# V of the second pass in seven products, its weight factors made on GpSimd, and x columns loaded one step ahead

## The chip, the cores and the metric

The kernel runs on one core of a Trainium2 chip. The metric is the device time of one execution in microseconds (us). The engines are named as in the profile: PE (TensorE, matmuls), PEld (its weight loads), DVE (VectorE), ACT (ScalarE), POOL (GpSimd) and SP (SyncE, which here issues all DMA transfers).

## The reference

One layer of a decoder trunk over 2048 tokens of width 1024, in fp32. The input projection has 6144 columns.

```python
h = rms_norm(x, g_pre) * (1 + scale) + shift
(pv, pg, hq, hf, hi, hg, mg_pool, mg_hgrn) = split(h @ w_in)   # 512, 512, then six times 1024
branch_a = (pooled(pv) * pool_scale * silu(pg)) @ w_pool_o
f = lb + (1 - lb) * sigmoid(hf);  q = silu(hq);  v = hi         # 8 heads of 128
o = rms_norm(hgrn2(q, 1 - f, v, log f), hgrn_norm_g)            # gated linear recurrence
branch_b = (o * silu(hg)) @ w_hgrn_o
y = (sigmoid(mg_pool) * branch_a + sigmoid(mg_hgrn) * branch_b) @ w_out
x = x + gate * rms_norm(y, g_post)
```

The stage that the change is mainly about is `v = hi`: h (2048x1024) times the 1024 columns of `w_in` that begin at `O_I`, called V below.

## The kernel before

**Passes and stages.** Two passes (`p`) over 1024 tokens each; a pass has two halves `t` of T = 512 tokens, and a half four tiles `tk` of P = 128. The stages of a pass follow each other: V, eight heads (in each three groups of products, `fq`, `m` and `gp`, and the small matmuls of the recurrence, the tiles `psa`, `PT`, `K`, `X` and `sq`), the projection of branch A (`psA`), that of branch B (`psB`), and y. During y of pass 0 the h of pass 1 is made: `x_cols` loads 256 columns of x in two transfers into `xc` and scales them on DVE, and `h_in` transposes a 128-column block of them on TensorE (`xT`). These steps wait in two lists, `early` (for half 0) and `late` (half 1). Two of `early` run after each part of y, and one of `late` after each part of y's second half; what is left of `late` runs in V of pass 1.

**A product.** fp32 products are made of three products of a rounded type: `split` casts the high part on ACT and subtracts it from the whole on DVE for the low part, and three matmuls of 128x512 sum hi·hi, hi·lo and lo·hi (two letters, as `hB` and `lB`, name the two parts).

**Weights.** `items` is the list of all weight tiles in the order of use. `take()` returns the next one (`whl`), and prepares up to four ahead (`LOOK`). In pass 0 a weight is loaded (`wr`), split, and where `keep` says so stored to DRAM (`scr`); in pass 1 `again` reloads the split tile, 512 KB, in one transfer.

**Seven products.** The input h is held as combinations of its halves and row blocks (`mv`; B11, B21, B12, B22 and T1 to T4, made from h by `h_mix`, whose calls are the list `mixes`), and the products of the heads and y of pass 1 use seven products on those combinations and on combinations of the weights, where plain halves would take eight. `rows7` does it for a stage of four weight tiles for each product: per product 4 weights x 4 tiles x 3 matmuls. y of pass 1 uses it (`FAST_Y`). Its weight combinations, the row factors, are made by `row_factors` in 56 small steps: it loads two blocks of rows, makes sums on DVE, splits each factor, and stores it to `scr` in DRAM. `htick`, which is called 21 times in a head (168 times in a pass), takes a step at every second call. V of both passes is computed without that, by `v_job`: 2 halves x 2 column groups x 8 weights x 4 tiles x 3 = 384 matmuls in pass 1.

**Order.** Each engine runs its instructions in program order. All DMA issues stand in one queue, SP's, also in order, so a store that waits for its data holds back the loads behind it. A scheduler places the instructions of the stages among one another, so small changes of a duration or a wait move rows on all engines.

Of the kernel before, what the change touches and what calls it, by code (L numbers as in the profile page):

```python
# [8 lines left out]
F32 = mybir.dt.float32  # L9
# [7 lines left out]
MUL, ADD, SUB, MAX, MIN = ALU.mult, ALU.add, ALU.subtract, ALU.max, ALU.min  # L17
# [3 lines left out]
D = 1024  # L21
# [10 lines left out]
O_PV, O_PG, O_Q, O_F, O_I, O_G, O_MP, O_MH = 0, 512, 1024, 2048, 3072, 4096, 5120, 6144  # L32
# [1 line left out]
MASK_W = P + 2 * 64 + 5 * NT * 64  # L34
NU = 76
GAP = 5
FAST_V, FAST_Y = False, True
KINDS = (("m", "gp"), ("gp", "m"))


# [30 lines left out]
def tile_block(ctx: ExitStack, tc: tile.TileContext, x, c, w_ada, b_ada, g_pre, g_post, w_in,  # L71
# [20 lines left out]
    def utile(name, dt=F32):  # L92
        return up.tile([P, T], dt, tag="u", name=name)

    def dram(name, shape):
        return dp.tile(shape, F32, name=name, tag=name)
# [10 lines left out]
    def store(key, dst, src):  # L107
        last["st"] = SP.dma_start(dst, src)

    def gated(dst, src, key=None):  # L110

        with after(last["st"]):
            return SP.dma_start(dst, src)
# [55 lines left out]
    scr = {}  # L169
    ready = []  # L170

    def split(src32, hi, lo):
        return A.copy(hi, src32), V.tensor_tensor(lo, src32, hi.bitcast(F32), op=SUB)  # L173

    def raw_load(name, srcs):
        raw = wrp.tile([P, T], F32, tag="wr", name=f"wr{name}")
# [6 lines left out]
    def item_split(name, raw):  # L183
        w = item_tile(name)
        split(raw, w[:, 0:T], w[:, T:2 * T])
        return w
# [60 lines left out]
            return [f0, f1, f2, f3, lambda: one(4, "21"), lambda: one(5, "12"), lambda: one(6, "22")]  # L247
        items.append((7, make))

    def row_factors(key, src):  # L250

        steps = []
        W = T // 2
        for i in range(4):
            for c0 in (0, W):
                r = {}

                def put(f, nm, i=i, c0=c0, r=r):
                    w = utile(f"rf{key}{f}{i}{c0}", F32R)
                    hi, lo = w[:, 0:W], w[:, W:T]  # L260
                    split(r[nm], hi, lo)
                    if (key, f, i) not in scr:
                        scr[key, f, i] = dram(f"scr_{key}_{f}_{i}", [P, 2 * T])
                    store((key, f, i), scr[key, f, i].rearrange("p (z n) -> p z n", z=2)[:, :, c0:c0 + W],
                          w.bitcast(F32).rearrange("p (z n) -> p z n", z=2))

                def ld(i=i, c0=c0, r=r):
                    a, b = utile(f"ra{key}{i}{c0}"), utile(f"rb{key}{i}{c0}")
                    for w, k in ((a, 2 * i), (b, 2 * i + 1)):
                        SP.dma_start(w.rearrange("p (z n) -> p z n", z=2),  # L270
                                     src[k * P:(k + 1) * P, :].rearrange("p (z n) -> p z n", z=2)[:, :, c0:c0 + W])
                    r.update({"11": a[:, 0:W], "21": a[:, W:T], "12": b[:, 0:W], "22": b[:, W:T]})

                def sums(r=r, i=i, c0=c0):
                    r["s1"] = utile(f"rs{key}{i}{c0}")[:, 0:W]
                    tt(r["s1"], r["21"], r["22"], op=ADD)
                    tt(r["21"], r["11"], r["21"], op=SUB)

                def sums2(r=r):
                    tt(r["11"], r["s1"], r["11"], op=SUB)  # L280

                def sums3(r=r):
                    tt(r["12"], r["12"], r["11"], op=SUB)

                def two(*fs, put=put):
                    for f in fs:
                        f() if callable(f) else put(*f)
                nop = lambda: None
                steps += [ld, nop, lambda two=two: two((0, "11"), (1, "12")),
                          lambda two=two, a=sums: two(a, (2, "s1")),  # L290
                          lambda two=two, a=sums2: two(a, (3, "11")),
                          lambda two=two, a=sums3: two((4, "21"), a),
                          lambda two=two: two((5, "12"), (6, "22"))]
        return steps
# [100 lines left out]
    def poolw_setup():  # L395
        pw = utile("pw_raw")
        SP.dma_start(pw.rearrange("p (g d) -> p g d", d=P), pool_w.rearrange("g c d -> c g d"))
        split(pw, pwh, pwl)
# [43 lines left out]
    def tt(o, a, b, op=MUL, e=None):  # L442
        return (e or V).tensor_tensor(o, a, b, op=op)  # L443
# [32 lines left out]
    def x_cols(p, t, i, cx):  # L476

        cs = []
        for half in range(2):
            xc = utile(f"xc{p}_{t}_{i}_{half}")  # L480
            v = xc.rearrange("p (a n) -> p a n", n=256)
            tok = p * 8 + t * NT + half * 2
            gated(v, x[tok * P:(tok + 2) * P, i * 256:(i + 1) * 256].rearrange("(a p) n -> p a n", p=P))
            for a in range(2):
                V.tensor_scalar(v[:, a, :], v[:, a, :], rst[:, tok + a:tok + a + 1], None, op0=MUL)
            cs.append(v)
        cx["xc"][t, i] = cs

    def h_in(p, t, k, cx):

        pt_ = px.tile([P, T], F32, tag="px", name=f"xT{p}_{t}_{k}")
        for tk in range(NT):
            if (t, k // 2) in cx["xc"]:
                src = cx["xc"][t, k // 2][tk // 2][:, tk % 2, (k % 2) * P:(k % 2 + 1) * P]
            else:
                src = cx["x"][t, tk][k // 4][:, (k % 4) * P:(k % 4 + 1) * P]
            PE.transpose(pt_[:, tk * P:(tk + 1) * P], src, ident)
        h32 = utile(f"h32_{p}_{t}_{k}")
        A.activation(h32, pt_, AF.Identity, bias=shv[:, k:k + 1], scale=scv[:, k:k + 1])
        cx["h32"][t, k] = h32  # L500
        nm = ("B11", "B21", "B12", "B22")[2 * t + k % 2]
        return part(p, nm, k // 2, h32, cx)

    def part(p, nm, i, src, cx):
        hi, lo = utile(f"h{nm}{p}_{i}", F32R), utile(f"l{nm}{p}_{i}", F32R)
        cx["mv"][nm, i] = (hi, lo)
        return split(src, hi, lo)
# [676 lines left out]
    for p in range(NPASS):  # L1184
# [50 lines left out]
        psa[:] = [ph.tile([P, T], F32, tag=f"ph{i}", name=f"psa{p}_{i}") for i in range(2)]  # L1235
        behind_heads = []
        if p == 0 and FAST_V:
            behind_heads += row_factors("v7", w_in[:, O_I:O_I + D])
        if p == NPASS - 1 and FAST_Y:
            behind_heads += row_factors("y7", w_out)  # L1240
        every = [0]

        def htick():
            tick()
            every[0] += 1
            if every[0] % 2 == 0:
                once(behind_heads)

        v_head(p, 0, cx)
        for h in range(NH):  # L1250
# [17 lines left out]
            steps = []  # L1268

            def tick_in():  # L1270
                htick()
                once(steps)

            quad("fq" + n, cx, fq, htick)
            active.extend(hgrn(p, h, t, cx) for t in range(2))
            htick()
            for i, kind in enumerate(KINDS[h == NH - 1]):
                if kind == "gp":
# [28 lines left out]
        if p + 1 < NPASS:  # L1307
            nx = cxs[p + 1]
            for t, steps in ((0, early), (1, late)):
                for i in range(4):  # L1310
                    steps.append(lambda p=p, t=t, i=i, nx=nx: x_cols(p + 1, t, i, nx))
                    for k in (2 * i, 2 * i + 1):
                        steps.append(lambda p=p, t=t, k=k, nx=nx: h_in(p + 1, t, k, nx))
        if p == NPASS - 1 and FAST_Y:
            y_fast(p, cx)
        for t in range(0 if p == NPASS - 1 and FAST_Y else 2):
# [32 lines left out]
```

## Time and profile before

| | us |
|---|---|
| median of 3 runs (lowest, highest) | 1829.64 (1827.5, 1830.42) |
| the profiled execution: its own time | 1831.51 |
| its span in the profile | 1829.7 |
| granted TensorE clock, mean | 0.996 |

| stage | from (us) | to (us) |
|---|---|---|
| start and V of pass 0 | 0 | 137 |
| heads of pass 0 | 137 | 700 |
| psA, psB of pass 0 | 700 | 846 |
| y of pass 0 | 846 | 944 |
| V of pass 1 | 944 | 1034 |
| heads of pass 1 | 1034 | 1600 |
| psA, psB of pass 1 | 1600 | 1740 |
| y of pass 1 and the tail | 1740 | 1830 |

Times are from the start of the span. In a row of a group, "x" is a count; in a row of the timeline the first two numbers are start and duration, and what stands in brackets is how long the engine was idle before and who ended it.

### The profile page before, as it was taken

To read this page: it belongs to the slowest core of one execution; us is meant where nothing else is said; L and a number is where in the kernel's file an instruction comes from. 1 tells how busy PE (TensorE), PEld (TensorE's weight loads), DVE (VectorE), ACT (ScalarE), POOL (GpSimd) and SP (SyncE) were. 2 spreads that over 40 slices of the span, in tenths; PEclk is the share of its full clock that TensorE was granted. 3 is DMA by queue.
4 is the path that set the end of the run, shared out by engine and by line. 5 is a ranking of instruction groups with operands and counts; after the bars stand their busy time and mean duration, and the time that the engine had idled before them with its cause. 6 is when DMAs were issued, how large, how long until landed. Compare 5 with 4: busy or idle time off the path is not lost.

```text
span 1829.7 us, 32049 instructions
## 1 busy us (share of the span) xinstructions
PE 1772.8 (97%) x12005; PEld 1449.7 (79%) x12005; DVE 1148.9 (63%) x2460; ACT 826.9 (45%) x1939; POOL 77.6 (4%) x136
## 2 busy tenths in 40 slices
PE   5899999999999999999999999999999999999997
PEld 4788878788788787887788878888788788888885
DVE  7577887787888884565443266566566555623446
ACT  4655656556666572223322345455455354310032
POOL 1100000000000100000000000000000000000001
PEclk9999999999999999999999999999999999999998
DMA  8698676777767669987887776876876755695457
GB/s 301 207 321 289 219 271 231 253 253 242 259 236 255 238 222 320 353 304 258 303 293 255 267 256 208 288 259 212 285 238 215 237 179 189 202 348 190 137 208 275
DMA packets 255540, 460.98 MB, mean 252 GB/s; under 512 B 20077, under 2 KB 129306, under 8 KB 255386
## 3 DMA queue, kind: packets, MB, share of 16 engines
q1 hardware_dynamic: 255386, 458.95, 73.1%
q8 instruction: 94, 1.54, 0.3%
q14 instruction: 60, 0.49, 0.1%
HBM read 271.70 MB, written 187.17 MB: 251 GB/s over the span
## 4 chain that ended last, share of the span: by engine, by line
PE 79%; ACT 5%; DMA 4%; DVE 4%; POOL 2%; issue 2%; SPq 0%; POOLq 0%; DVEq 0%; ACTq 0%
PE psB L325 9%; PE psV L325 8%; PE pagp L325 7%; PE pafq L325 7%; PE pam L325 5%; PE pefq L325 5%; PE psA L325 4%; PE pegp L325 4%; PE psy L325 3%; PE pem L325 3%; PE psa L325 3%; PE pbfq L325 2%; PE pdfq L325 2%; PE pdm L325 2%; PE pbm L325 2%; PE pbgp L325 2%
## 5 line engine op out<-in xcount | busy, mean ns | idle before, releaser
L173 DVE TENSOR_TENSOR whl<-wr,whl 128x512 fp32r<-128x512 f32 x210 | 144.1, 690 | 85.7 <-ACT whl L173 84.4
L173 ACT CAST whl<-wr 128x512 fp32r<-128x512 f32 x210 | 130.0, 620 | 127.7 <-PE psB L325 26.5
L325 PE MATMUL psV<-whl,hB 128*128 128x512 f32 x512 | 162.6, 400 | 1.4 <-ACT V L840 1.4
L325 PE MATMUL psB<-Gh,whl 128*128 128x512 f32 x512 | 158.6, 390 | 0.0
L325 PEld LDWEIGHTS psV<-whl,hB 128*128 128x128 f32 x512 | 97.7, 193 | 21.5 <-ACT V L840 1.7
L631 DVE COPY_PREDICATED PT<-mask,psa 128x256 f32<-128x256 uint8 x160 | 86.2, 548 | 44.3 <-PE psa L325 44.2
L325 PEld LDWEIGHTS psB<-Gh,whl 128*128 128x128 f32 x512 | 96.1, 188 | 20.4 <-issue 0.5
L325 PE MATMUL psV<-whl,lB 128*128 128x512 f32 x256 | 101.2, 397 | 0.0
L325 PE MATMUL psB<-Gl,whl 128*128 128x512 f32 x256 | 100.0, 391 | 0.0
L325 PE MATMUL pam<-hT,whl 128*128 128x512 f32 x256 | 87.4, 402 | 0.0
L325 PE MATMUL pagp<-hT,whl 128*128 128x512 f32 x256 | 86.2, 397 | 0.0
L325 PE MATMUL psA<-Ph,whl 128*128 128x512 f32 x256 | 82.6, 397 | 3.4 <-DMA Ph<-Pd 1.7
L325 PE MATMUL pafq<-hT,whl 128*128 128x512 f32 x256 | 84.0, 389 | 0.0
L443 DVE TENSOR_TENSOR K<-K,TT 128x256 f32<-128x256 f32 x192 | 81.4, 425 | 0.7 <-PE psa L325 0.7
L325 PE MATMUL psy<-whl,mgh 128*128 128x512 f32 x256 | 80.6, 395 | 0.7 <-DVE y L443 0.7
L325 PEld LDWEIGHTS psa<-X,K 128*32 128x32 f32 x2816 | 50.0, 110 | 30.0 <-issue 19.2
L325 PE MATMUL psa<-X,K 128*32 128x48 f32 (+2 forms) x2816 | 60.7, 208 | 2.7 <-DVE PT L625 2.7
L443 DVE TENSOR_TENSOR sm<-psB,sm 128x512 f32<-128x512 f32 x32 | 22.0, 688 | 63.8 <-PE psB L325 62.4
L625 DVE COPY_PREDICATED PT<-mask,psa 128x256 f32<-128x256 uint8 (+1 forms) x96 | 52.0, 542 | 12.0 <-PE psa L325 11.9
L325 PEld LDWEIGHTS psA<-Ph,whl 128*128 128x128 f32 x256 | 47.6, 188 | 15.0 <-DMA Ph<-Pd 3.5
L325 PEld LDWEIGHTS psV<-whl,lB 128*128 128x128 f32 x256 | 49.1, 192 | 10.5
L325 PEld LDWEIGHTS pagp<-hT,whl 128*128 128x128 f32 x256 | 48.0, 188 | 10.9 <-issue 0.2
(437 smaller groups left out, 4532.2 us busy)
## 6 DMA issues: line engine op xcount, KB each, us to landing
wr<-in_w_in_dram SPq DMA_DIRECT2D x122, 256.0 KB, 4.7
whl<-scr_y SPq DMA_DIRECT2D x44, 512.0 KB, 4.7
sm<-Sd SPq DMA_DIRECT2D x64, 256.0 KB, 4.6
whl<-scr_v SPq DMA_DIRECT2D x32, 512.0 KB, 4.2
scr_y<-rfy SPq DMA_DIRECT2D x56, 256.0 KB, 3.2
wa<-in_w_ada_dram SPq DMA_DIRECT2D x32, 256.0 KB, 5.4
x<-in_x_dram SPq DMA_DIRECT2D x32, 256.0 KB, 5.4
Vd<-V SPq DMA_DIRECT2D x32, 256.0 KB, 2.4
```

The lines of the kernel that those rows point to most:

```text
L173: return A.copy(hi, src32), V.tensor_tensor(lo, src32, hi.bitcast(F32), op=SUB)
L325: PE.matmul(o, lhsT=l, rhs=r, start=start, stop=stop, skip_group_check=True)
L443: return (e or V).tensor_tensor(o, a, b, op=op)
L625: V.copy_predicated(dst.rearrange("p (c a) b -> p c a b", c=NT), m.unsqueeze(1).broadcast_to(shp), src.unsqueeze(2).broadcast_to(shp))
L631: V.copy_predicated(dst.rearrange("p (c q) a b -> p c q a b", c=NT), m, src.rearrange("p c (a b) -> p c a b", b=b).unsqueeze(2) .broadcast ...
```

## The change

It has three parts.

1. V of pass 1 is computed by `rows7`, with 336 matmuls where 384 were. Its row factors, 28 tiles of 512 KB, are made during the heads of pass 0 by `row_factors`, with the low parts and the sums on GpSimd (`G`); the casts stay on ACT. For that there are 16 loads and 56 stores of 256 KB, 56 casts on ACT, and 88 operations of 128x256 on GpSimd. The 16 stores of 512 KB by which V of pass 0 kept its split weights for pass 1 go, and the 32 reloads in V of pass 1 become 28 reloads of factors. The `mixes`, which ran one at a time through the second half of V, run within the second of the seven products (B21), and the `late` steps that are left within the first (B11).
2. `htick` takes a step of the factors at two of five calls, where it was one of two, for V's factors in pass 0 and y's in pass 1.
3. The columns of x in y of pass 0 are loaded one step ahead of the transposes that use them (`ORDER_IN`).

```diff
-FAST_V, FAST_Y = False, True
+FAST_V, FAST_Y = True, True
+ORDER_IN = ("x0", "x1", "h0", "h1", "x2", "h2", "h3", "x3", "h4", "h5", "h6", "h7")
...
-    def split(src32, hi, lo):
-        return A.copy(hi, src32), V.tensor_tensor(lo, src32, hi.bitcast(F32), op=SUB)
+    def split(src32, hi, lo, e=None):
+        return A.copy(hi, src32), (e or V).tensor_tensor(lo, src32, hi.bitcast(F32), op=SUB)
...
-    def row_factors(key, src):
+    def row_factors(key, src, e):
...
-                    split(r[nm], hi, lo)
+                    split(r[nm], hi, lo, e)
...
-                    tt(r["s1"], r["21"], r["22"], op=ADD)
-                    tt(r["21"], r["11"], r["21"], op=SUB)
+                    tt(r["s1"], r["21"], r["22"], op=ADD, e=e)
+                    tt(r["21"], r["11"], r["21"], op=SUB, e=e)
...
-            behind_heads += row_factors("v7", w_in[:, O_I:O_I + D])
+            behind_heads += row_factors("v7", w_in[:, O_I:O_I + D], G)
         if p == NPASS - 1 and FAST_Y:
-            behind_heads += row_factors("y7", w_out)
+            behind_heads += row_factors("y7", w_out, V)
...
-            if every[0] % 2 == 0:
+            if every[0] % 5 in (1, 3):
                 once(behind_heads)
...
-                for i in range(4):
-                    steps.append(lambda p=p, t=t, i=i, nx=nx: x_cols(p + 1, t, i, nx))
-                    for k in (2 * i, 2 * i + 1):
-                        steps.append(lambda p=p, t=t, k=k, nx=nx: h_in(p + 1, t, k, nx))
+                for z in ORDER_IN:
+                    if z[0] == "x":
+                        steps.append(lambda p=p, t=t, i=int(z[1]), nx=nx: x_cols(p + 1, t, i, nx))
+                    else:
+                        steps.append(lambda p=p, t=t, k=int(z[1]), nx=nx: h_in(p + 1, t, k, nx))
```

The code that `FAST_V` turns on in pass 1:

```python
def v_got(n, t, tk, src):
    vt = src
    if (n, t) == (1, 0):
        vt = utile(f"V{p}_{t}_{n}_{tk}")
        A.copy(vt, src)
    store("Vd", cx["Vd"][:, t * NT + tk, n * T:(n + 1) * T], vt)

def v_step(nm, i):
    if nm == "B11":
        for _ in range(len(late) if i == 2 else 2):
            once(late)
    elif nm == "B21":
        for _ in range(2 if i == 2 else 1):
            once(mixes)

rows7(f"V{p}", cx["mv"], v_got, v_step)
```

Three places show how the rows move. The first is GpSimd in the first heads of pass 0. Before, its queue holds the mask, then the small operations of x's statistics (`rst`) and of the HGRN norm (`ss`):

```order
L136 CAST mask_98<-mask_i1024_694 128x512
L453 TENSOR_SCALAR rst_147<-xss8_2072 128x1
L443 TENSOR_TENSOR rst_147<-rst_147,mh_114 128x1
L741 TENSOR_SCALAR ss0_0_0_2436<-ss0_0_0_2436 128x4
L443 TENSOR_TENSOR ss0_0_0_2436<-ss0_0_0_2436,mh_114 128x4
```

In the changed kernel the low parts of the factors (`rfv7`) and four sums in a row (`rsv7`, `rav7`, `rbv7`) stand there; this is the second set of factors:

```order
L444 TENSOR_TENSOR rst_147<-rst_147,mh_114 128x1
L174 TENSOR_TENSOR rfv700256_2157<-rav70256_1970,rfv700256_2157 128x256
L174 TENSOR_TENSOR rfv710256_2161<-rbv70256_1971,rfv710256_2161 128x256
L444 TENSOR_TENSOR rsv70256_2280<-rav70256_1970,rbv70256_1971 128x256
L444 TENSOR_TENSOR rav70256_1970<-rav70256_1970 128x256
L444 TENSOR_TENSOR rav70256_1970<-rsv70256_2280,rav70256_1970 128x256
L444 TENSOR_TENSOR rbv70256_1971<-rbv70256_1971,rav70256_1970 128x256
L174 TENSOR_TENSOR rfv720256_2283<-rsv70256_2280,rfv720256_2283 128x256
L174 TENSOR_TENSOR rfv730256_2338<-rav70256_1970,rfv730256_2338 128x256
L174 TENSOR_TENSOR rfv740256_2554<-rav70256_1970,rfv740256_2554 128x256
L742 TENSOR_SCALAR ss0_0_0_2472<-ss0_0_0_2472 128x4
```

Nine of GpSimd's operations have moved in between `rst` and the first `ss`, which was next behind it.

The second place is TensorE in an odd head of pass 0, at the change from one head's recurrence to the next head's `fq` products. Before, three small matmuls of the recurrence (`psa`) stand between the matmuls with `whl116` and those with `whl117`:

```order
L325 MATMUL pafq0_4_4599<-lB110_3_553,whl116_4462 128x512
L325 MATMUL pafq0_4_4599<-hB110_3_553,whl116_4462 128x512
L325 MATMUL psa0_0_1372<-X32_0_3_0_4557,K0_3_0_3982 32x32
L325 MATMUL psa0_0_1372<-sq0_3_0_3961,K0_3_0_3982 32x64
L325 MATMUL psa0_0_1372<-X32_0_3_0_4557,K0_3_0_3982 32x32
L325 MATMUL pefq0_4_4620<-hT10_0_1004,whl117_4486 128x512
```

In the changed kernel `pefq` follows directly there, and the same three stand behind the last matmuls with `whl120`:

```order
L326 MATMUL pafq0_4_4763<-lT30_3_1214,whl120_4785 128x512
L326 MATMUL pafq0_4_4763<-hT30_3_1213,whl120_4785 128x512
L326 MATMUL psa0_0_1340<-X32_0_3_0_4715,K0_3_0_4112 32x32
L326 MATMUL psa0_0_1340<-sq0_3_0_4091,K0_3_0_4112 32x64
L326 MATMUL psa0_0_1340<-X32_0_3_0_4715,K0_3_0_4112 32x32
```

They have moved back by 48 matmuls of 128x512.

The third place is the start of V of pass 1, SP's queue first, then DVE's, in the changed kernel (`xr` is a row of the output, `yss` the scale of the norm of y, and `xc1_1_3` the last columns of x for pass 1):

```order
L196 DMA whl257_10320<-scr_v7_0_1_2956 128x1024
L109 DMA out_0_dram<-xr0_1_0_0_10252 128x512
L196 DMA whl258_10403<-scr_v7_0_2_4449 128x1024
L114 DMA xc1_1_3_0_10378<-in_x_dram 128x2x256
L114 DMA xc1_1_3_1_10382<-in_x_dram 128x2x256
L196 DMA whl259_10405<-scr_v7_0_3_5886 128x1024
```

```order
L1020 TENSOR_SCALAR yss0_1_3_10168<-yss0_1_3_10168 128x1
L486 TENSOR_SCALAR xc1_1_3_0_10378<-xc1_1_3_0_10378,rst_147 128x256
L1029 SCALAR_TENSOR_TENSOR xr0_1_3_0_10264<-y0_1_0_3_10171,yss0_1_3_10168,xr0_1_3_0_10264 128x512
L1029 SCALAR_TENSOR_TENSOR xr0_1_3_1_10265<-y0_1_1_3_10360,yss0_1_3_10168,xr0_1_3_1_10265 128x512
L486 TENSOR_SCALAR xc1_1_3_0_10378<-xc1_1_3_0_10378,rst_147 128x256
L486 TENSOR_SCALAR xc1_1_3_1_10382<-xc1_1_3_1_10382,rst_147 128x256 x2
```

TensorE uses these columns (`xT1_1_6`) behind the second weight of the first product; before, their loads came later and their use 48 matmuls further on, behind the sixth weight. On SP they now stand behind the first output store alone, and on DVE the first scaling stands ahead of the last two sums of y.

More of the change, by code (lines that the diff above doesn't have):

```diff
@@ L275, in sums @@
                     r["s1"] = utile(f"rs{key}{i}{c0}")[:, 0:W]
-                    tt(r["s1"], r["21"], r["22"], op=ADD)
-                    tt(r["21"], r["11"], r["21"], op=SUB)
+                    tt(r["s1"], r["21"], r["22"], op=ADD, e=e)
+                    tt(r["21"], r["11"], r["21"], op=SUB, e=e)
                 def sums2(r=r):
-                    tt(r["11"], r["s1"], r["11"], op=SUB)
+                    tt(r["11"], r["s1"], r["11"], op=SUB, e=e)
                 def sums3(r=r):
-                    tt(r["12"], r["12"], r["11"], op=SUB)
+                    tt(r["12"], r["12"], r["11"], op=SUB, e=e)
                 def two(*fs, put=put):
```

## The prediction

> **What bounds the kernel now.** I read the page first, then TensorE's waits, then a table of the span by stage, then the chain of work. The page's first rows say that TensorE is the bound:
>
> ```profile
> span 1829.7 us, 32049 instructions
> PE 1772.8 (97%) x12005; PEld 1449.7 (79%) x12005; DVE 1148.9 (63%) x2460; ACT 826.9 (45%) x1939; POOL 77.6 (4%) x136
> ```
>
> So a removed matmul shows in the time, and anything else only if TensorE comes to wait. The stages (columns: window, length, busy PE, PEld, DVE, ACT, POOL, granted clock, DMA share, GB/s) are a head of pass 0 (354 to 426), psA of pass 0, V of pass 1, a head of pass 1, and y of pass 1 with the tail:
>
> ```profile
> 354.00:426.00 72.00, 70.77 (x577) 58.05 (x576) 60.02 (x132) 43.64 (x106) 3.68 (x6) 1.00 0.74 259
> 700.00:757.00 57.00, 53.00 (x317) 43.27 (x316) 22.30 (x45) 14.95 (x47) 3.27 (x6) 1.00 0.98 344
> 944.00:1034.00 90.00, 90.00 (x406) 74.49 (x405) 31.36 (x53) 23.99 (x42) 1.78 (x4) 1.00 0.77 260
> 1168.00:1240.00 72.00, 71.51 (x578) 58.41 (x577) 44.59 (x111) 36.53 (x96) 2.41 (x4) 1.00 0.75 253
> 1740.00:1830.00 90.00, 76.42 (x336) 62.63 (x335) 48.52 (x82) 26.70 (x60) 6.42 (x9) 0.95 0.68 245
> ```
>
> The reader should see two things. V of pass 1 has no gap (90.00 of 90), at a clock of 1.00. And DVE is busy 60 of 72 us in a head of pass 0, but 45 in a head of pass 1, where it makes y's factors besides: pass 0 splits its weights itself, pass 1 reloads them. TensorE's waits from 137 to 700, then 757 to 944, then after 1740 (total, times, longest):
>
> ```profile
> PE pdm L325 <- ACT pdm L549: 3.1, 6, 0.6
> PE psa L325 <- DVE PT L625: 2.7, 3, 1.4
> ...
> PE xT L497 <- DVE xc L485: 2.2, 3, 0.8
> ...
> PE rxy1B L325 <- ACT hT4m L173: 0.8, 1, 0.8
> ```
>
> **The change, part by part.** *V in seven products.* The chain of work gives matmuls in long unbroken pieces (start, length, what, count):
>
> ```profile
> 1652.95 87.04 PE psB L325 x384
> 1739.99 10.88 PE ray L325 x48
> ...
> 1772.63 20.41 PE ray L325 x90
> 1795.22 9.11 PE rxy1B L325 x39
> ```
>
> 87.04/384 = 0.2267 us for a 128x512 matmul, and 48 make 10.88. V falls from 384 matmuls to 7 x 4 x 4 x 3 = 336: **-10.9**. Its traffic is that of y of pass 1, the same seven products: an item of 512 KB for each 12 matmuls, before as after. That stage stood still once, 0.8 us at a product's border (1795.22, for the split of a factor); V has the same borders: **+0.8** (0 to 2). The mixes, which make the combinations of the rows of h, come in four groups. In DVE's rows of V before, one group begins so:
>
> ```profile
> 970.02 0.68 DVE L443 TENSOR_TENSOR t<-h,h 128x512 f32<-128x512 f32 x1
> 970.74 0.69 DVE L443 TENSOR_TENSOR h<-h,h 128x512 f32<-128x512 f32 x1
> ```
>
> A group has four such subtractions and four lo parts, so all have 4 x 8 x 0.69 = 22 us of DVE work. They stood over the second half of V; now they are put into the second product, which lasts 10.9 us, and the third, T1, wants the last of them in its last weight, some 8 us after it begins. 22 us of work in some 19: a wait of 3 us, of which eleven matmuls of T2 (2.5 us), which stand before T1's last weight, cover most. **+0.7** (0 to 3).
>
> *x columns one step ahead.* In y of pass 0 the three waits of xT on xc go: **-2.2** (-2.2 to 0). What is late next: the last columns, xc1_1_3, are loaded with y's last product, and stand in SP's queue behind an output store that waits for DVE. The rows of DVE, then SP, then PE at that place (start, length):
>
> ```profile
> 944.24 0.74 DVE L1028 SCALAR_TENSOR_TENSOR xr<-y,yss,xr 128x512 f32<-128x512 f32 x1
> ...
> 947.23 4.07 DVE L1028 SCALAR_TENSOR_TENSOR xr<-y,yss,xr 128x512 f32<-128x512 f32 x6 [0.51 <-POOL yss L443]
> 956.45 0.62 DVE L485 TENSOR_SCALAR xc<-xc,rst 128x256 f32<-128x256 f32 x2 [3.70 <-DMA xc<-in_x_dram]
> ...
> 945.01 0.34 SPq L108 DMA_DIRECT2D out_dram<-xr  x1
> 945.45 0.39 SPq L195 DMA_DIRECT2D whl<-scr_v  x1
> 951.06 0.42 SPq L113 DMA_DIRECT2D xc<-in_x_dram  x1
> ...
> 944.02 0.60 PE L497 MATMUL xT<-ident,xc 128*128 128x128 f32 x4
> 944.37 0.72 PE L325 MATMUL psV<-whl,hB 128*128 128x512 f32 x2
> ```
>
> The store goes when the first output is summed (944.98), a weight load follows it (945.45), then the columns: issued at about 945.9 and 946.4, and landed 5.4 us later (951.06 to 956.45), so at 951.3 to 951.8. On DVE the scaling of the first stands ahead of the last two sums of y (2 x 0.68) and the rest of the scaling (0.31 each): ready at about 953.9. TensorE wants them after 24 matmuls and 8 transposes from 944.0 on, so 5.44 + 0.7 later, at 950.2. A new wait of 3.7 us; I take **+3** (0 to 4).
>
> *The factors on GpSimd.* 56 steps at two of five hook calls take 140 of the 168 calls of the heads, 140/168 of 563 us = 469 us, or 6.5 heads of 72 us. Rows that price them (GpSimd's groups: busy us, mean ns; then y's factors of pass 1, the same operations on 128x256, ns min/median/max):
>
> ```profile
> L443 POOL TENSOR_TENSOR xr<-rcy,xr 128x512 f32<-128x512 f32 x1 | 1.3, 1261 | 0.8 <-ACT rcy L1060 0.8
> L136 POOL CAST mask<-mask_i 128x512 uint8<-128x512 int32 x3 | 2.1, 738 | 0.0
> L173 ACT CAST rfy<-ray x24: 395/402/427, 1053.8 to 1401.1; 128x256 fp32r<-128x256 f32 x24
> L173 DVE TENSOR_TENSOR rfy<-ray,rfy x24: 414/420/455, 1054.5 to 1401.9; 128x256 fp32r<-128x256 f32 x24
> L108 SPq DMA_DIRECT2D scr_y<-rfy x56: 518/528/729, 1055.0 to 1410.2; - x56
> ```
>
> - GpSimd: 88 operations, each between half of 1.26 and all of it; I take 0.7, so 62 us in 469, on an engine with 4 us of work in a head. None of it is on the path by itself.
> - ACT: 56 casts x 0.40 = 22.4 us, 3.4 in each head, beside 44 of 72. 16 of them stand right behind a sum that GpSimd makes, and everything behind them on ACT waits along: 16 x 0.7 = 11 us, 1.7 in a head. ACT keeps over 20 us idle in a head.
> - SP: 16 loads and 56 stores, 72 x 0.53 = 38 us of issue; each store waits for a GpSimd subtraction, and the weight loads of the head stand behind it. A weight tile is ordered four items ahead.
> - DMA: 16 loads and 56 stores of 256 KB are 18.9 MB, +40 GB/s on 259; 344 GB/s were reached from 700 to 757. The 16 stores of 512 KB that kept V's splits go: 8 MB less in pass 0's V.
> - DVE: no instruction is added, but the two engines were seen to disturb each other once, where GpSimd cast the mask:
>
> ```profile
> 67.30 0.88 DVE L469 TENSOR_SCALAR x<-x,rst 128x512 f32<-128x512 f32 x2 [0.84 <-POOL rst L443]
> ...
> 69.55 1.56 DVE L469 TENSOR_SCALAR x<-x,rst 128x512 f32<-128x512 f32 x2 [0.76 <-POOL rst L443]
> 71.03 1.09 DVE L173 TENSOR_TENSOR whl<-wr,whl 128x512 fp32r<-128x512 f32 x1
> 72.24 0.69 DVE L173 TENSOR_TENSOR lB<-h,hB 128x512 fp32r<-128x512 f32 x1
> ...
> 69.47 2.11 POOL L136 CAST mask<-mask_i 128x512 uint8<-128x512 int32 x3
> ```
>
> DVE lost 0.68 + 0.40 = 1.08 us beside 2.11 us of GpSimd, half. By that 62 us of GpSimd cost DVE 31 us, 4.8 in a head: 65 of 72 busy. In the other direction GpSimd's power for the HGRN norm (`ss`) queues behind up to four sums, 2.8 us, and ACT waits for it already:
>
> ```profile
> ACT on L746 <- POOL ss L443: 13.6, 12, 1.4
> ```
>
> These delays have cover (DVE 7 us, ACT 20 us in a head), but the cover is uneven: the psa waits above came while DVE worked off a queue. I give the heads **+3** for all of this; the bounds are 0 and 9, which is the 3.1 + 2.7 of TensorE's present waits there and half as much again; +3 is the half of the present ones.
>
> *Order in the heads.* The 2.7 of psa waits come from three blocks that stand early among fq's matmuls in the odd heads 1, 3 and 5; in the changed order they stand 48 matmuls, 10.9 us, later, more than the longest wait: **-2.7** (-2.7 to 0). *Factors of y* at the new rate: same work over a longer stretch of a stage with 27 us of DVE idle in 72: 0.
>
> Sum: -10.9 + 0.8 + 0.7 - 2.2 + 3 + 3 - 2.7 = **-8.3 us**. The profiled execution took 1831.51 with a span of 1829.7; the median of the runs is 1829.64, 1.9 below the former. The difference applied to the median gives 1821.3 us, and 1821.4 for the span.
>
> A rule speaks against this change. The Trainium skill, "SBUF — State Buffer", section "SBUF: two separate sides", says that DVE and GpSimd share a port pair as an exclusive lock: an operation of DVE with two SBUF inputs and one of GpSimd that reads SBUF exclude each other for the whole instruction. The trace agrees by half: 1.08 of 2.11 us. By the rule 62 us would be taken from DVE, not 31, and with the heads at +16 (rival 1) the sum would be +5 instead of -8.3.
>
> **The rivals.** (1) *DVE becomes the bound: slower.* If each GpSimd operation stops DVE for all its length, DVE loses 62/6.5 = 9.5 us in a head and needs 69.5 of 72; if they also last 1.26 us (111 us in all, 17 in a head), 77 of 72. It decides from 12 us in a head on, the idle time that DVE has now: with 17, each head grows by 5, 33 us in all, and the time is 1829.6 - 11.3 (the sum without the heads) + 33 = 1851. With 9.5, 2.5 us short of it, the uneven cover makes TensorE wait some 2.5 us in a head, 16 in all: 1834. For it: 1.26 in the only two-input row. Against it: only half was lost at 69.5. (2) *ACT waits for GpSimd: no change.* At 346.64 a GpSimd operation that takes 0.30 took 1.49 beside a dense DVE:
>
> ```profile
> 275.69 0.30 POOL L453 TENSOR_SCALAR rst<-xss 128x1 f32<-128x1 f32 x1 [36.20 <-ACT jx L451]
> ...
> 346.64 1.49 POOL L453 TENSOR_SCALAR rst<-xss 128x1 f32<-128x1 f32 x1 [34.80 <-ACT jx L451]
> ```
>
> If each of the 88 is held up by 1.2 us, a cast behind two sums waits 3.8 us, 16 of them 61 us; if a fifth of that reaches TensorE through late weights, the heads cost 12 instead of 3, and the time is 1829.6 - 11.3 + 12 = 1830. Against it: ACT is idle 28 us in a head. (3) *The heads cost nothing, and the columns land in time:* -10.9 - 2.2 - 2.7 + 0.8 = -15, so 1814.6. For it: in pass 1 DVE made the same factors and TensorE's busy time in a head was 71.5 of 72. Against it: DVE has 15 us more work in a head of pass 0.
>
> **How the numbers follow.** My forecast (a gain of 4 to 12, 1818 to 1826) 0.57; (3) 0.14; (2) 0.14; (1) 0.15. Two runs of this kernel can differ by about 0.2%, 3.7 us, which I take as the least that can be told: faster means under 1826. Faster: 0.57 + 0.14 = 0.71, less 0.03 for the forecast's upper edge, 0.68. Same (1826 to 1833): 0.03 + 0.14 = 0.17, plus 0.01 of (1). Slower: 0.14. The range takes in (3), (2) and the start of (1), 1814 to 1832; most of (1) is left out and a little below (3), under 2 in 10.
>
> **What would show it.** V of pass 1 at 336 matmuls and 76 to 81 us, with one wait of xT on xc of 3 to 4 us some 6 us after its start, and none on the mixes above 3. No wait of psa on PT in heads 1, 3, 5; no wait of xT in y of pass 0. In a head of pass 0: GpSimd 12 to 15 us busy, its 128x256 operations 0.6 to 1.3 us, DVE 62 to 67 us, ACT 47, TensorE within 0.5 us of its present busy share. Wrong would be: DVE at 70 or more in a head, or TensorE waiting for `whl`, `PT` or `pdm` by over 1.5 us in each head; then rival (1) or (2) holds. If V itself does not shrink by 48 matmuls, the first step falls.

## The result and the profile after

The changed kernel takes 1847.89 us (median of 4 runs, 1846.13 to 1852.67), the kernel before 1828.57 us beside it: a ratio of 1.0102, 95% interval 1.0089 to 1.0115. It is 19 us slower, where 8 us faster was forecast.

The page of the changed kernel begins:

```profile
span 1845.9 us, 32378 instructions
PE 1770.4 (96%) x11957; PEld 1445.8 (78%) x11957; DVE 1180.9 (64%) x2476; ACT 841.7 (46%) x1991; POOL 163.2 (9%) x224
```

48 matmuls fewer (11957 for 12005), but PE's busy time fell by 2.4 us only, where 10.9 were due. The table by stage says where. For each stage the window runs from its first matmul to that of the next; first the kernel before (heads of pass 0, y of pass 0, V of pass 1, first head of pass 1), then the changed one (columns as in the prediction: window, length, busy PE, PEld, DVE, ACT, POOL, clock, DMA share, GB/s):

```profile
133.37:699.06 565.69, 559.80 (x4474) 458.08 (x4472) 465.04 (x1023) 347.98 (x827) 29.49 (x42) 1.00 0.71 248
846.22:944.37 98.15, 95.11 (x437) 76.80 (x436) 43.44 (x86) 34.85 (x69) 2.74 (x5) 1.00 0.83 289
944.37:1033.04 88.67, 88.67 (x399) 73.34 (x398) 30.99 (x52) 23.31 (x41) 1.74 (x3) 1.00 0.78 261
1033.04:1096.11 63.07, 62.10 (x450) 49.89 (x448) 30.64 (x77) 26.88 (x57) 0.00 (x0) 1.00 0.82 272
```

```profile
131.95:724.39 592.44, 568.94 (x4474) 464.65 (x4472) 486.46 (x1023) 366.05 (x883) 114.91 (x130) 0.98 0.77 269
871.75:966.02 94.27, 93.52 (x434) 76.78 (x432) 43.22 (x86) 34.66 (x68) 2.74 (x5) 1.00 0.87 301
966.02:1046.89 80.87, 79.74 (x353) 64.22 (x352) 41.30 (x68) 21.04 (x37) 1.65 (x3) 1.00 0.77 260
1046.89:1111.76 64.87, 62.15 (x450) 49.90 (x448) 30.73 (x77) 26.86 (x57) 0.00 (x0) 1.00 0.84 265
```

The start is 1.4 us shorter (133.37 to 131.95), y 3.9, V 7.8. The first head of pass 1 is 1.8 us longer, and the heads of pass 0 are **26.75 us** longer. With 0.8 us in the rest that is the 16.2 us between the spans. In the heads PE runs the same 4474 matmuls. It stands still 23.5 us instead of 5.9 (length less busy time), and its busy time grew by 9.1 us at a granted clock of 0.98. DVE is busy 21.4 us longer with the same 1023 instructions.

What TensorE waits for in the heads of the changed kernel (total, times, longest):

```profile
PE pdm L326 <- ACT pdm L550: 17.2, 6, 4.5
PE pw L326 <- ACT pmh L174: 4.3, 4, 2.3
```

The psa waits are gone, as forecast; the waits of pdm, 3.1 us before, are 17.2. One of them, in head 6, in the order in which it comes about; GpSimd, then ACT, then TensorE (start, length, idle before and releaser in brackets):

```profile
614.76 4.42 POOL L174 TENSOR_TENSOR rfv<-rav,rfv 128x256 fp32r<-128x256 f32 x1 [8.79 <-ACT rfv L174]
619.27 0.32 POOL L742 TENSOR_SCALAR ss<-ss 128x4 f32<-128x4 f32 x1
619.67 1.02 POOL L444 TENSOR_TENSOR ss<-ss,mh 128x4 f32<-128x4 f32 x1
622.47 0.19 POOL L742 TENSOR_SCALAR ss<-ss 128x4 f32<-128x4 f32 x1 [1.78 <-ACT junk L741]
...
620.73 0.37 ACT L747 ACTIVATE on<-po,ss 128x128 f32<-128x128 f32 x1 [2.85 <-POOL ss L444]
623.79 1.15 ACT L747 ACTIVATE on<-po,ss 128x128 f32<-128x128 f32 x4 [0.85 <-POOL ss L444]
625.41 0.61 ACT L550 COPY pdm<-pam 128x512 f32<-128x512 f32 x1
...
626.07 0.63 PE L326 MATMUL pdm<-hT,whl 128*128 128x512 f32 x1 [3.42 <-ACT pdm L550]
```

The same place in the kernel before, a head earlier:

```profile
525.67 0.37 ACT L746 ACTIVATE on<-po,ss 128x128 f32<-128x128 f32 x1 [1.41 <-POOL ss L443]
528.74 1.14 ACT L746 ACTIVATE on<-po,ss 128x128 f32<-128x128 f32 x4 [0.85 <-POOL ss L443]
530.05 0.61 ACT L549 COPY pdm<-pam 128x512 f32<-128x512 f32 x1
...
530.71 0.50 PE L325 MATMUL pdm<-hT,whl 128*128 128x512 f32 x1 [0.44 <-ACT pdm L549]
```

`pdm` is a copy of `pam`, and the last of the seven products of the m group is summed onto it; TensorE wants it 2.7 us after `pam` is done. In ACT's queue the copy stands behind the eight scalings `on` of the HGRN norm of the head before, and these wait twice for a power on GpSimd (`ss`). Before, the copy came just too late, by 0.4 to 0.6 us in each of six heads. Now a GpSimd operation on a factor, which takes 0.73 us undisturbed, lasts 4.42 us, `ss` stands behind it, `on` waits 2.85 us instead of 1.41, and TensorE 3.42.

That is one entrance of several. Of the six waits, only this one and that of head 1 (heads count from 0) had `ss` behind a factor. The longest, in head 5, came about ahead of the norm's squares (`junk`, whose sums `ss` needs); ACT, then TensorE:

```profile
536.14 0.41 ACT L662 COPY X<-sq 128x256 f32<-128x256 f32 x1 [1.76 <-DVE sq L444]
540.44 0.60 ACT L810 ACTIVATE sgm<-pbm 128x512 f32<-128x512 f32 x1 [2.22 <-POOL rfv L174]
540.94 0.27 ACT L741 ACTIVATE junk<-po 128x128 bf16<-128x128 f32 x1
...
538.28 0.50 PE L326 MATMUL pam<-hT,whl 128*128 128x512 f32 x1 [0.41 <-ACT c12m L532]
548.59 0.80 PE L326 MATMUL pdm<-hT,whl 128*128 128x512 f32 x1 [4.54 <-ACT pdm L550]
```

and in the kernel before:

```profile
522.07 0.28 ACT L740 ACTIVATE junk<-po 128x128 bf16<-128x128 f32 x1
...
524.54 0.50 PE L325 MATMUL pam<-hT,whl 128*128 128x512 f32 x1
```

The first square started 2.5 us ahead of these `pam` matmuls before, and now 2.7 us behind them: `X` waited for DVE's `sq`, and `sgm` for a GpSimd operation on a factor (by its place, for the tile that this one still held; the trace shows the wait and not the reason). Counted from the start of these `pam` matmuls, the first matmul with `pdm` came 14.0 us later than before in the six heads together, and 11.2 of that were there when ACT had done the squares of the norm's first half. Ahead of them `X` waited 7.7 us in all for DVE, where it had not waited before, and `sgm` 2.2 us for GpSimd and, in head 4, 1.1 us for the store of a factor. So the delay enters ACT's queue through GpSimd's queue, through DVE and through `sgm`, and most of it comes out at `pdm`: 14.1 of the 17.6 us by which TensorE stands still longer.

Behind such a wait the matmuls run slow. The clock (before the last two columns) in the 3.9 us from that matmul on, and in the 6 us after:

```profile
626.07:630.00 3.93, 3.93 (x10) 3.14 (x11) 3.60 (x7) 2.99 (x7) 0.66 (x1) 0.57 0.94 335
630.00:636.00 6.00, 6.00 (x34) 4.72 (x34) 4.32 (x7) 3.46 (x6) 0.00 (x0) 1.00 0.89 345
```

### The profile page after: what moved, and what is told of

It reads as the page before. It is cut to its first block, busy times and chain, and to the rows that moved or that the text cites. A ratio compares the mean times of both kernels' runs of the same rounds, so it can differ in the third digit from the quotient of the medians.

```text
span 1845.9 us, 32378 instructions
## 1 busy us (share of the span) xinstructions
PE 1770.4 (96%) x11957; PEld 1445.8 (78%) x11957; DVE 1180.9 (64%) x2476; ACT 841.7 (46%) x1991; POOL 163.2 (9%) x224
## 4 chain that ended last, share of the span: by engine, by line
PE 64%; DMA 4%; DVE 3%; ACT 3%; issue 2%; POOL 2%; SPq 0%; POOLq 0%; DVEq 0%; ACTq 0%
PE psB L326 9%; PE pagp L326 5%; PE pafq L326 5%; PE psy L326 4%; PE psA L326 4%; PE pegp L326 4%; PE pefq L326 3%; PE pam L326 3%; PE pdm L326 2%; PE pem L326 2%; PE psa L326 2%; PE raV L326 2%; PE pbfq L326 2%; PE ray L326 2%; PE pbgp L326 2%
## 5 line engine op out<-in xcount | busy, mean ns | idle before, releaser
L174 DVE TENSOR_TENSOR whl<-wr,whl 128x512 fp32r<-128x512 f32 x210 | 149.6, 717 | 83.6 <-ACT whl L174 72.5
L174 ACT CAST whl<-wr 128x512 fp32r<-128x512 f32 x210 | 129.7, 620 | 118.1 <-PE psB L326 17.6
L326 PE MATMUL psV<-whl,hB 128*128 128x512 f32 x256 | 82.8, 406 | 1.2 <-ACT V L841 1.2
L742 POOL TENSOR_SCALAR ss<-ss 128x4 f32<-128x4 f32 x32 | 9.2, 287 | 765.7 <-ACT junk L741 765.4
L326 PE MATMUL pdm<-hT,whl 128*128 128x512 f32 x128 | 48.9, 446 | 21.5 <-ACT pdm L550 21.5
L326 PEld LDWEIGHTS psV<-whl,hB 128*128 128x128 f32 x256 | 49.3, 195 | 11.5 <-ACT V L841 1.4
```

What stands on the lines that cost most here:

```text
L174: return A.copy(hi, src32), (e or V).tensor_tensor(lo, src32, hi.bitcast(F32), op=SUB)
L326: PE.matmul(o, lhsT=l, rhs=r, start=start, stop=stop, skip_group_check=True)
L742: G.tensor_scalar(ss, ss, 1.0 / P, EPS, op0=MUL, op1=ADD)
```

## The experiments

Theory A: what the heads lost goes through the norm's way over GpSimd and ACT's queue to pdm. Theory B: it goes through the casts, the stores in SP's queue and the traffic (B2: SP's queue alone). Theory C: DVE, disturbed by GpSimd, is short of time. "Loss" is the difference of a kernel's median to that of the kernel before measured beside it; the changed kernel's is +19.3 us. The tables by stage and the waits are from one profiled run of each kernel.

### Which part of the change: e1, e2, e3

e1 (`e1_factors_dve`):

```diff
-            behind_heads += row_factors("v7", w_in[:, O_I:O_I + D], G)
+            behind_heads += row_factors("v7", w_in[:, O_I:O_I + D], V)
```

> V's factors are made as in the changed kernel, but their low parts and sums on DVE instead of GpSimd; casts, loads, stores and the rate of the steps stay. Theory A (GpSimd's queue): factor operations on GpSimd, lengthened beside DVE, hold back the power of the HGRN norm (ss), behind which ACT waits with the copy pdm that TensorE needs at once; each wait above some 2 us is then followed by matmuls at half the clock. By A the waits of pdm fall from 21.5 us to about 4, DVE has 88 x 0.42 = 37 us more (66 of 72 in a head), and the time is 1820 to 1830. Theory B (the casts on ACT, the stores in SP's queue and the DMA traffic delay the heads, whoever makes the sums): pdm still waits 15 us or more and the time is 1840 to 1850. Theory C (DVE is short of time in the heads, by the shared port): worse than the changed kernel, 1850 or more.

Measured: 1825.9 us, ratio 0.9976 (0.9963 to 0.9989), 3.8 us faster than before.

e2 is the kernel before with the third part of the change alone (`ORDER_IN` and the loop over it).

> The kernel before with only the new order of the x columns. From the trace of the changed kernel, where y of pass 0 was 3.9 us shorter: 3 to 4 us faster than before, 1825, under all theories, with no wait of xT in y; if the 3.9 us came from other parts (less traffic, other order), no change, 1828.

Measured: 1827.58 us, ratio 0.9993 (0.9983 to 1.0004). Its y was 4.4 us shorter in the trace, its first head of pass 1 0.9 longer and V 0.6, so some 2 us remain and the interval does not part them from none. Its start was 1.4 us shorter as well, so that was not the removed stores.

e3 takes GpSimd's part out and leaves the rest (sums and low parts omitted, high part stored twice; one place of five shown):

```diff
-                    split(r[nm], hi, lo, e)
+                    if e is G:
+                        A.copy(hi, r[nm])
+                    else:
+                        split(r[nm], hi, lo, e)
```

> The changed kernel without GpSimd's part of the factors: the sums and the low parts of V's factors are left out (the store writes the high part twice), so V of pass 1 is computed from wrong factors; the 56 casts, 16 loads and 56 stores stay. Theory A: the heads of pass 0 return to before (pdm waits 3 to 4 us in all, GpSimd 4 us busy in a head), so 1829 - 1 - 4 - 8 + 2 = about 1817. Theory B: the heads still lose 15 us or more, 1835 to 1845. Theory C: as A, 1817.

Measured: 1823.05 us, ratio 0.9961 (0.9947 to 0.9974). The heads of pass 0 in the table by stage of e1:

```profile
129.97:699.58 569.61, 559.98 (x4474) 459.00 (x4472) 489.76 (x1111) 365.51 (x883) 30.32 (x42) 1.00 0.80 280
```

and of e3:

```profile
130.54:697.96 567.42, 559.37 (x4473) 458.49 (x4471) 462.68 (x1023) 365.62 (x883) 29.78 (x42) 1.00 0.80 281
```

565.7 before, 567.4 without GpSimd's part: casts, loads, stores and some 30 GB/s more cost the heads 1.7 us net, so theory B falls, but for B2, since no store of e3 waits for GpSimd. The 1.7 hide two things: the psa waits fell from 2.7 to 0.5 us, and pdm waited 7.4 us where it was 3.1 (8.6 in e1), so the casts alone already lengthen the way to pdm. e1 refutes C as a shortage of DVE's time: in it DVE is busy 489.8 us in the heads, more than in the changed kernel (486.5), and the heads are 22.8 us shorter. To give 88 operations to GpSimd relieved DVE of 3.3 us, since the 21.4 us by which its other instructions grew take the place of the 24.7 that the operations cost there.

### What in GpSimd's part: e6, e7, e9, e8, e5

e6 and e7 are e3 with 88 operations on GpSimd, whose results nobody uses, at the places of the real ones, in e6 of the same shape, in e7 as small powers (one place of four shown):

```diff
+                        G.tensor_tensor(dum[:, 0:W], r[nm], hi.bitcast(F32), op=SUB)                            # e6
+                        G.tensor_tensor(dum[:, 0:NT], hi.bitcast(F32)[:, 0:NT], mh[:, 0:NT], op=ALU.pow)        # e7
```

> As e3, but 88 GpSimd operations of 128x256 stand at the places of the real ones, read the same tiles and write a scratch tile: the stores, the casts and the products do not wait for them (V of pass 1 again from wrong factors). What is left of GpSimd's part is its queue ahead of ss, the shared access to SBUF with DVE, and tiles that stay taken until it has read them. e3 took 1823.1, the changed kernel 1847.9. Theory A/C (GpSimd's queue ahead of the norm, and DVE slowed): most of the 25 us return, 1838 to 1848. Theory B2 (what costs is that SP's queue waits with the factors' stores for GpSimd, and the weight loads stand behind it): close to e3, 1822 to 1828.

> As e6, but the 88 operations are powers of 128x4, which take 1.0 us each of GpSimd's time and read almost nothing: GpSimd's queue ahead of ss stays as full, the access to SBUF is gone. Theory A (queue): as e6, 10 us or more above e3. Theory C (DVE and GpSimd disturb each other in SBUF): as e3, 1821 to 1826, with DVE's busy time in the heads back at 463 us. Theory B2: as e3.

Measured: e6 1840.61 us, ratio 1.0066 (1.0042 to 1.0090); e7 1830.75 us, ratio 1.0009 (0.9995 to 1.0022). The heads of e7:

```profile
130.60:705.86 575.26, 563.35 (x4474) 461.35 (x4472) 463.88 (x1023) 365.28 (x883) 131.41 (x130) 0.99 0.79 278
```

and of e6:

```profile
131.84:717.60 585.76, 565.96 (x4473) 462.76 (x4471) 483.51 (x1023) 365.56 (x883) 117.02 (x130) 0.99 0.78 273
```

e7 occupies GpSimd longest (131 us) and leaves DVE at 463.9: its 7.8 us above e3 are GpSimd's queue (and the tiles that wait for it) without DVE; `ss` stood behind an added power in four of its six heads. Operations of 128x256 that read SBUF lengthen DVE's time by 20 us, and cost 10.5 us more. So both halves, the queue (A) and the disturbance (C), were there; what they act on is mainly pdm still (15.1 us of waits in e6's heads, 11.9 in e7's).

e9 issues each factor's store one step later (`held`):

```diff
-                    store((key, f, i), scr[key, f, i]...
+                    held.append(((key, f, i), scr[key, f, i]...
```

> The changed kernel with each factor's store put into SP's queue one step later (two or three hook calls, some 8 us), so that GpSimd is done when the store's turn comes; y's factors of pass 1 alike. Theory B2: SP no longer waits for GpSimd, 10 us or more come back, 1828 to 1836. Theories A and C: no or little change, 1842 to 1850.

Measured: 1844.07 us, ratio 1.0076 (1.0049 to 1.0102), a loss of 14.6 us, some 5 us less than the changed kernel's, which the two intervals do not part. So by the medians B2 makes at most 5 of the 19 us. e6 and e9 spread over 9 and 10 us from run to run, and the profiled run is the fastest of each, so how the last 8 us between e6 and the changed kernel divide stays open.

e8 keeps the steps out of the m products:

```diff
-            if every[0] % 5 in (1, 3):
+            if p == 0:
+                if (every[0] - 1) % 21 in (0, 2, 4, 6, 14, 16, 18, 20):
+                    once(behind_heads)
+            elif every[0] % 5 in (1, 3):
```

> The changed kernel with the real factors, but in pass 0 the 56 steps are taken at 8 of the 21 hook calls of a head, none of them from the start of the m products to their end, where the norm of the head before stands. Theory A (queue): the waits of pdm fall to 5 us or less and the time to 1825 to 1832. Theories C and B2: the wait moves to the fq and gp products, 1840 to 1848.

Measured: 1846.36 us, ratio 1.0087 (1.0066 to 1.0108), against theory A as it was worded. The first `ss` of no head stood behind a factor now, and pdm still waited 11.0 us; waits of pd, pw, psa and pafq (other tiles of the heads) on ACT and DVE made 10 us more: the work had moved to where other copies have little room.

e5 takes pdm's copy in pass 0 away from ACT:

```diff
-        A.copy(d, a)
+        if name.startswith("m0"):
+            V.tensor_copy(d, a)
+        else:
+            A.copy(d, a)
```

> The changed kernel with the copy pdm in the m products made by DVE instead of ACT, so that it no longer stands behind the norm in ACT's queue; GpSimd's work stays. Theory A: the waits of pdm on ACT are gone, some return as waits of DVE or of the projection behind it; 15 to 20 of the 27 us that the heads lost come back, 1828 to 1833. Theory C: DVE is the shortage, so the copy comes late from DVE too, 1845 or more. Theory B: as A for the pdm wait, but other waits in the heads stay at 5 us or more.

Measured: 1846.15 us, ratio 1.0093 (1.0072 to 1.0114); theory A's figure was wrong again. TensorE's longest waits in its heads:

```profile
PE pw L326 <- ACT pmh L174: 11.9, 4, 6.7
PE pdm L326 <- DVE pdm L551: 4.4, 3, 2.6
PE pdgp L326 <- ACT pdgp L553: 2.1, 1, 2.1
```

The copy now stood in DVE's queue, behind what GpSimd lengthened there, and the longest wait, 6.7 us, came from a raw weight that was loaded late (DVE stood 6.54 us for it). After e5 and e8 theory A was in doubt, so the chain was measured by itself.

### The chain by itself: e12 and f_e12

e12 is the kernel before with nothing but one more small operation in the norm of pass 0:

```diff
         G.tensor_scalar(ss, ss, 1.0 / P, EPS, op0=MUL, op1=ADD)
+        if p == 0:
+            s2 = sp.tile([P, NT], F32, tag="s2", name="s2" + n)
+            tt(s2, ss, mh[:, 0:NT], op=ALU.pow, e=G)
```

> The kernel before (V by eight products, no factors of V), with one more power of 128x4 on GpSimd, whose result nobody uses, ahead of the power of each HGRN norm in pass 0: 1.0 us of GpSimd's time, almost nothing read. Theory A (the norm's way over GpSimd, then ACT's queue, then pdm, has no room): pdm waits 1 us longer for the first half and 1 us more for the second in each of six heads, 12 us in all, and where a wait passes 2.3 us the matmuls behind it run slow for 1.4 to 2.2 us: 1841 to 1852. Rival (GpSimd's time in itself is covered, only wide operations and late stores cost): at most 3 us, 1829 to 1833.

Measured: 1847.13 us, ratio 1.0100 (1.0085 to 1.0115). 16 operations of 1.0 us on an engine that is idle over nine tenths of the time cost 18 us; pdm's six waits grew to 2.6 to 2.8 us each. The `f_` kernels change only the order in ACT's queue of the kernel in their name:

```diff
-        A.copy(d, a)
+        state["d"] = A.copy(d, a)
...
-            A.activation(on[:, cc * P:(cc + 1) * P], po[:, cc, :], AF.Copy, scale=ss[:, cc:cc + 1])
+            with after(state.get("d") if p == 0 else None):
+                A.activation(on[:, cc * P:(cc + 1) * P], po[:, cc, :], AF.Copy, scale=ss[:, cc:cc + 1])
```

> e12 (one more power on GpSimd ahead of each norm) with the eight scalings (on) of the norm put behind the copy pdm in ACT's queue in pass 0, all else alike. Theory A: the transposes that use the norm's result stand 12 matmuls behind, so 3 us of room appear; pdm's waits go to 0 and all of e12's 18 us come back and 3 more, 1825 to 1828. If the loss had another way (DVE, clock of itself): 1840 or more.

> The changed kernel with the same order in ACT's queue (pdm ahead of the norm's scalings). Theory A alone: pdm's waits in pass 0 and the slow matmuls behind them go, 17 of 27 us, and the time is 1826 to 1832. Theory B2/C (wide operations slow DVE, late stores hold back the weights): other waits take their place as in e5, 1838 to 1846.

> e1 (V's factors on DVE) with the same order in ACT's queue. pdm's waits in the heads of pass 0 (about 8 us) go: 1817 to 1821, faster than all before it. If DVE, busy 62 of 72 us, delays something else: 1823 to 1826.

> The kernel before with the same order in ACT's queue: pdm's 3.1 us of waits in pass 0 go, 1825 to 1827; no change if something behind the norm becomes late.

| kernel | median us | ratio to before (95%) | without the order |
|---|---|---|---|
| f_before | 1821.54 | 0.9951 (0.9934 to 0.9968) | 1 |
| f_e12 | 1823.88 | 0.9962 (0.9948 to 0.9975) | 1.0100 |
| f_after | 1825.51 | 0.9971 (0.9958 to 0.9985) | 1.0102 |
| f_e1 | 1812.75 | 0.9906 (0.9879 to 0.9934) | 0.9976 |

The heads of pass 0 in the table by stage, of e12:

```profile
130.29:713.05 582.76, 564.14 (x4473) 461.37 (x4471) 465.06 (x1023) 347.77 (x827) 43.72 (x56) 0.99 0.69 241
```

of f_e12:

```profile
131.95:689.73 557.78, 557.78 (x4474) 458.64 (x4472) 464.65 (x1023) 346.74 (x827) 46.04 (x56) 1.00 0.73 252
```

of f_before:

```profile
130.72:688.50 557.78, 557.78 (x4473) 458.64 (x4471) 464.76 (x1023) 346.83 (x827) 29.99 (x42) 1.00 0.73 252
```

of f_after:

```profile
131.85:702.98 571.13, 562.08 (x4473) 459.13 (x4471) 485.11 (x1023) 365.01 (x883) 117.11 (x130) 1.00 0.80 280
```

and of f_e1:

```profile
130.55:690.59 560.04, 558.09 (x4474) 458.37 (x4472) 490.76 (x1111) 364.03 (x883) 26.79 (x42) 1.00 0.81 285
```

This settles where the loss comes out. With pdm ahead of the norm's scalings, e12's additional power costs the heads nothing: 557.78 us with it and without, and TensorE never stands. The changed kernel gets 21.3 of its heads' 26.75 us back (592.44 to 571.13), though the profiled run of f_after is the slowest of its ten. It stays 13.4 us above f_before, and 11 of these are GpSimd's own, since with the work on DVE (f_e1) it is 2.3; they show as waits of other tiles (pw 4.5 us, pafq 1.8, pdm 1.0) and one stretch at half the clock. The order also takes 7.9 us out of the heads of the kernel before, more than the 3.1 of pdm's waits: with the changed order no wait of psa is left either (2.7).

### Rate, place and the best version: e14, e11, e10, f_e1_both

All are e1 with another place for the steps: e14 `every[0] % 2 == 0`, e11 the places of e8, e10 34 steps in the heads and the rest in psB.

> e1 (V's factors on DVE) with the old rate of the steps, one of two hook calls instead of two of five, in both passes. If the slower rate helps the heads, they lose some us more than e1's 3.9: 1827 to 1832. If it matters to nothing, 1825.9 as e1.

> e1 (V's factors on DVE) with the steps of pass 0 kept out of the m products, as in e8. If the casts and DVE's work ahead of the norm are what e1's heads still lose (3.9 us, pdm waits 13.9 us in both passes), 2 to 4 us faster than e1, 1822 to 1824; if the work only moves, 1825 to 1829.

> e1 with about 34 of V's 56 steps in the heads and the rest in psB of pass 0, where DVE was busy 56 of 89 us and ACT 19. If the heads' loss goes with the work there, 2 us faster than e1, 1823 to 1825; if the stores, at 298 GB/s of traffic in psB, hold back sm's loads, slower than e1, 1827 to 1832.

Measured: e14 1826.64 us, ratio 0.9982 (0.9969 to 0.9995), and e11 1826.24, 0.9979 (0.9968 to 0.9990): with the work on DVE, the rate and the place in the heads make no difference that the runs can show. e10 took 1845.48, 1.0089 (1.0069 to 1.0109), far beyond what was expected: in psB a weight came late three times, and two stretches of 6.8 us at half the clock came with that. What made it late stays open.

```profile
PE psB L326 <- ACT whl L174: 9.9, 3, 5.8
```

f_e1_both has the order in pass 1 too (`state.get("d")` in both passes).

> f_e1 with the norm's scalings behind pdm in pass 1 as well. pdm's waits in pass 1, some 4 to 5 us in all, go: 1807 to 1810; if they have cover or something else takes their place, 1812 as f_e1.

Measured: 1808.12 us, ratio 0.9887 (0.9869 to 0.9906). It is the best version: V in seven products, its factors on DVE, pdm ahead of the norm, 21 us faster than the kernel before.

## Why the prediction was wrong

**The step that failed** is the end of "The factors on GpSimd": "These delays have cover (DVE 7 us, ACT 20 us in a head)", and its term, +3 with a bound of 9. The heads grew by 26.75 us although the 2.7 of psa went, so the term measured about +29. Its place was quoted: `PE pdm <- ACT pdm`, six waits, and `ACT on <- POOL ss`, 12 waits. They were read by their size: the bound was the present waits and half as much again. But a wait of 0.4 to 0.6 us at the same place in each of six heads says that the chain that ends there has no room at all, and DVE's `sq`, ACT's queue and GpSimd's queue are links of it. The idle share of ACT says nothing of an instruction that stands behind a wait in ACT's own queue. Then came the clock, for which the prediction had no term: 17.6 us of waiting more came with 9.1 us more of busy time for the same matmuls, half as much again. The sign that it gave for being wrong, waits of `pdm` over 1.5 us, did appear: there were five such, in six heads that waited 2.9 us in the mean.

**What held.** The prices of the work were right in the main. GpSimd's 88 operations took 88.5 us (62 forecast), 1.0 us each in the mean, and DVE grew by 21.4 (31 forecast).

**Rival (1)** had the sign, and not the mechanism: DVE was not short in sum, 486 of 592 us, and e1 with more on DVE is faster; what it had right is that GpSimd makes single results of DVE late. **Rival (2)** named ACT waiting for GpSimd, but for the 16 casts behind sums, and called the loss 12 us; ACT's longest waits for GpSimd were for `ss`.

**The other terms.** V: 48 matmuls less, as forecast; its stage fell by 7.8, since PE's busy time in it fell by 8.9, where 10.9 were due (the 2 us between stay open), and 1.1 us of standing still came in. The waits in it were 0.7 us for the x columns (+3 forecast; their loads were issued 0.3 us after V began, where 1.5 were reckoned), 0.3 for a weight (+0.8) and none for the mixes (+0.7). y: -3.9 where -2.2 was forecast. psa: gone, -2.7. y's factors at the new rate: 0 within the noise, by e14. Not foreseen was a wait of the first fq products of pass 1 for a reloaded weight, 2.5 us where it was 0.7 before:

```profile
PE pbfq L326 <- DMA whl<-scr_('fq', 0)_3_1358: 2.5, 1, 2.5
```

With the order of ACT's queue mended and the factors on DVE (f_e1), the seven products with the other two parts are worth 8.8 us against f_before: the gain that was forecast is there once the heads do not pay for it.

## What to carry to other kernels

A short wait of the bounding engine that comes back at the same place in every round marks a chain without room: what delays any queue on it just then, however idle that engine is, counts in full (e12), and more where the clock falls behind the wait. Look at what stands in front of the needed instruction in its own queue, and move it ahead of work that waits for others; that one order was worth 9 us alone and 24 us with the change. Here, giving work on tiles in SBUF to GpSimd hardly took it off DVE: it saved DVE 3 us of 25.

## What the runs showed of the hardware that had not been expected

*Operations of DVE with two inputs and wide ones of GpSimd excluded each other, instruction by instruction, at the two places shown.* The prediction took "half" from one place. In head 6 the GpSimd operation at 614.76 ended at 619.18, 0.69 us after DVE's unbroken run of two-input operations ended and one that reads PSUM began (618.49):

```profile
614.74 0.69 DVE L236 TENSOR_TENSOR wr172s<-wr,wr 128x512 f32<-128x512 f32 x1
...
617.89 0.69 DVE L241 TENSOR_TENSOR wr<-wr172s,wr 128x512 f32<-128x512 f32 x1
618.49 0.75 DVE L626 COPY_PREDICATED PT<-mask,psa 128x512 f32<-128x512 uint8 x1
```

In the other direction a DVE operation that came 0.03 us after a GpSimd one waited it out, 1.25 us instead of 0.69:

```profile
532.46 0.74 POOL L444 TENSOR_TENSOR rav<-rav 128x256 f32<-128x256 f32 x1
...
532.49 1.25 DVE L174 TENSOR_TENSOR whl<-wr,whl 128x512 fp32r<-128x512 f32 x1
```

This is the rule of the Trainium skill, "SBUF — State Buffer", section "SBUF: two separate sides": the pair of ports is a lock, held by whoever starts first for the whole instruction. The trace agrees with it at both places. In sum each held up the other about as much: GpSimd's 88 operations took 88.5 us where 88 x 0.73 = 64 were due undisturbed, and DVE's time grew by 21 us, a third of the 64; e7's small operations lengthened it by none.

*The clock fell after waits of 2.3 us and more, not after each.* Waits of 2.3, 2.7, 3.3, 3.4 and 4.5 us in the changed kernel were followed by 3 to 6 us of matmuls of 128x512 at 0.43 us each instead of 0.227; those of 1.2 and 2.1 were not. In e12, with six waits of 2.60 to 2.78 us, three were. The clock after the first of these (2.62) and after the second (2.78):

```profile
240.57:246.00 5.43, 5.43 (x28) 4.59 (x29) 5.43 (x11) 4.66 (x10) 0.00 (x0) 1.00 0.57 226
314.79:320.00 5.21, 5.21 (x21) 4.32 (x22) 3.29 (x7) 3.29 (x7) 0.00 (x0) 0.71 0.58 231
```

The Trainium skill, "TensorE: Matmul & The Clock Gate", section "HAM oscillation — how this bites in real kernels", warns of idle gaps above about 3.4 us; here 2.3 us was enough at one place, and 2.62 was not at another; the measurement decides. Nothing here shows what tells these places apart.
